# A two-layer decoder trunk: copying L's blocks out with ScalarE, moving bonus and gate into the units, and taking GpSimd's products to VectorE

## The chip, the cores and the metric

The kernel runs on one core of a Trainium2 chip as a single program. The metric is the device time of one execution in microseconds (us). A core has four engines that compute (TensorE for matrix products and transposes, VectorE, ScalarE and GpSimd for elementwise work), a fifth, SyncE, whose queue issues the transfers, and 16 DMA engines that carry them. Each engine works through its own list of instructions in order and waits for the others by semaphores.

## What is computed

The reference is a trunk of two layers over 256 tokens of width 2048, all in float32. The change touches only the mixer of the even layer. Its group A is an RWKV-7 recurrence with 16 heads of 64, its group B a sliding-window attention with 16 query heads on 2 key heads, and one output projection takes both.

```python
h = x @ e_w_in                        # r, k, v | decay, a, gate | q, k, v of attention
h = h + (token_shift(h) - h) * mu     # group A only
def wkv7_step(state, inp):            # one token: a_t = -kk, b_t = kk * a
    sa = einsum('bhij,bhj->bhi', state, a_t)
    state = state * w_t + sa[..., None] * b_t + v_t[..., None] * k_t
    return state, einsum('bhij,bhj->bhi', state, r_t)
y = scan(wkv7_step)
y = (y - mean(y)) * rsqrt(var(y) + WKV_GN_EPS) * gn_w + gn_b
bonus = sum(r * k * r_k, -1) * v      # per head
ya = (y + bonus) * g                  # the gate
yb = swa_sink_attention(q, k, v, sinks)
mix = concatenate([ya, yb]) @ e_w_out # then residual, LayerNorm, SwiGLU, LayerNorm, PLE
```

The odd layer (differential attention) and all that follows the even layer's output projection are the same before and after.

## The kernel before

Weights come from HBM in float32, two slabs of 128 rows by 512 columns at a time (a `raw` tile, 128x1024). `split_weights` makes two fp32r tiles of each: ScalarE casts `hi` (L109), VectorE subtracts `lo` (L110). The activations are split in the same way, and each product of the reference is three TensorE products here (`hi*xh`, `lo*xh`, `hi*xl`: L133 to L135 in `gemm`, L155 to L159 in `gemm_t`), called weight products below. So no weight product can run before ScalarE and then VectorE have done their part.

`wkv_operands` prepares the recurrence. Feature blocks f = 0 to 7 (two heads each) come in two halves, c = 0 and 1: per block the scaled operands `ar` and `bk` (L586 to L590), and after each second block the strictly lower 32x32 diagonal blocks of the matrix of `bk` times `ar`, written through the mask `m32` into the zeroed tile `blk` (L608: 16 masked copies of 32x128 per half, straight from PSUM). GpSimd makes three of the products of a block (L569, L589, L591). Then come the v projection (two gemms), the token shift of v by DMAs from `v` to `vs` (L627 to L629) with its two GpSimd operations and one VectorE operation per tile (L631 to L633), the mean removal (L638 to L640), and on GpSimd the bonus, the bias `gn_b`, the gate and the weight `gn_w` over whole tiles of 128x512 (L650 to L654). VectorE meanwhile transposes `blk` and inverts 128 triangular blocks of 32x32 by forward substitution (L665, L667: 60 operations), which gives `Tc` and `TTc`.

`wkv_chunks` is a generator of eight units: four groups of four heads, each with two chunks c of 128 tokens. A unit forms the masked matrices `lm4` (L706 on TensorE, L707 on VectorE, four of them), assembles the inverse `TT` from 32x32 blocks (GpSimd copies L711, TensorE L716 and L723, VectorE copies L719 and L726), and solves for `u` and `y` by a chain that passes between TensorE, ScalarE and VectorE (L729 to L781). L729 is its first product with `vs`; it and L741 need the v path and the inverse. A unit ends with the variance (L788 to L790), the scaling (L792), and two GpSimd operations that put in `gn_w` times gate and add to bonus (L793, L794).

`even_layer` writes four units, then the attention's projections (`swa_project`) and eight attentions (`swa_attend`), four of them between units. The order of the instructions on each engine is not the written one alone: a scheduler interleaves the lists, so weight products stand in the gaps of the units. Tiles come from pools, and a tile that takes over another's place waits for its last reader. In the end the eight heads' results are turned (`split_t`) and multiplied by `w_out` in two halves, first `ya`, whose sums wait in two tiles of 128x2048, then `yb`.

Of the kernel before, what the change touches and what calls it, by code (L numbers as in the profile page):

```python
# [9 lines left out]
F32 = mybir.dt.float32  # L10
# [8 lines left out]
P = 128  # L19
# [28 lines left out]
class Trunk:  # L48
# [24 lines left out]
    def more(self):  # L73

        pool = lambda n, b: self.ctx.enter_context(self.tc.tile_pool(name=n, bufs=b))
        self.rings.append(pool("wx", 3))
        self.rp = pool("rows", 2)
        self.ep = pool("emb", 1)
# [85 lines left out]
    def split_t(self, src, tag, pool):  # L164

        nc = self.nc
        ps = self.sm.tile([P, 2, SEQ], F32, name="s")
# [197 lines left out]
def even_layer(T, a, src):  # L365
# [4 lines left out]
    with ExitStack() as ctx:  # L370
        ev = ctx.enter_context(tc.tile_pool(name="ev", bufs=1))
        with tc.tile_pool(name="prep", bufs=1) as pr, T.psum(4, 4):
            ops, xT = wkv_operands(T, src, w_in, a, ev, pr)
            y = ops[-1]
        with tc.tile_pool(name="pairs", bufs=2) as pp, T.psum(2, 4, 2):
            units = wkv_chunks(T, ev, pp, *ops)
            for _ in range(4):
                next(units)
# [3 lines left out]
            yb = [None] * 4  # L382
            for u in range(4):
                next(units)
                swa_attend(T, pp, u, yb, *qkv)
            next(swa)
            for f in range(4, 8):
                swa_attend(T, pp, f, yb, *qkv)
            ya = [T.split_t([y[t][:, j * 256:(j + 1) * 256] for t in range(NT)], f"x{j}", T.xt) for j in range(4)]
            sums = [pp.tile([P, D], F32, name=f"lmat{t}", bufs=1) for t in range(NT)]  # L390
            for c in range(4):
                acc = T.gemm(ya, w_out, c * 512, rows=range(0, 8, 2))
                for t in range(NT):
                    nc.scalar.copy(out=sums[t][:, c * 512:(c + 1) * 512], in_=acc[t])
            x = T.load_x(src)
            for c in range(4):
                acc = T.gemm(yb, w_out, c * 512, rows=range(8, 16, 2), tail=2 if c == 3 else 0)
                for t in range(NT):
                    cs = slice(c * 512, (c + 1) * 512)
                    nc.vector.scalar_tensor_tensor(out=x[t][:, cs], in0=x[t][:, cs], scalar=ALPHA,  # L400
                                                   in1=sums[t][:, cs], op0=ALU.mult, op1=ALU.add)
# [4 lines left out]
def wkv_operands(T, src, w_in, a, ev, pr):  # L406
# [106 lines left out]
    late = tc.tile_pool(name="late", bufs=1)  # L513
# [12 lines left out]
    bview = blk.rearrange("p t (g c f r) -> p g r f c t", c=2, f=2, r=2)  # L526
    c2 = lambda u: u.rearrange("p (c t) -> p c t", t=P)
    ft = lambda n: lt.tile([P, SEQ], F32, name=n, bufs=4)
    bs = [pr.tile([P, AH], F32, name=f"bs{t}") for t in range(NT)]
    for c in range(2):  # L530
# [30 lines left out]
        for i in range(4):  # L561
# [7 lines left out]
            nc.gpsimd.tensor_tensor(out=bv, in0=kk[i], in1=av[i], op=ALU.mult)  # L569
# [19 lines left out]
            nc.gpsimd.tensor_tensor(out=bk[:, :, 0], in0=c2(bv), in1=en, op=ALU.mult)  # L589
            nc.vector.tensor_tensor(out=bk[:, :, 1], in0=c2(k[i]), in1=en, op=ALU.mult)  # L590
            nc.gpsimd.tensor_tensor(out=kk[i], in0=r, in1=k[i], op=ALU.mult)  # L591
# [472 lines left out]
```

## Time and profile before

| | before |
|---|---|
| median of 3 runs | 2655.54 us (2654.8 to 2657.75) |
| the profiled execution | 2654.55 us |
| its span, first to last instruction | 2652.9 us |
| TensorE busy | 2585.4 us, 97% of the span |
| VectorE, ScalarE, GpSimd busy | 1492.6, 1138.9, 121.9 us |
| granted TensorE clock, mean | 0.983 |

All durations below are from the profiled execution; what lies outside its span is 1.65 us. The granted clock is given as a share of 2.4 GHz; at 1.2 GHz, the lower of the two levels, it is 0.5, and a stretch with 0.71 has been partly at one and partly at the other. A weight product's busy time overlaps that of the next one, so counts of products are multiplied with the distance between two starts. The part that the change touches ends at about 563 us of the span.

### The profile page before, as it was taken

What the parts mean: (1) busy time and instruction counts of PE and PEld (TensorE: products, weight loads), DVE (VectorE), ACT (ScalarE), POOL (GpSimd) and SP (SyncE); (2) the same over time, 40 slices, a digit from 0 to 9 for tenths busy, and PEclk for the clock granted to TensorE, in tenths of its full rate; (3) what the DMA queues carried; (4) which work ended last, traced back from release to release, by engine and by line L of the source; (5) the groups of instructions that cost most, each with busy time, mean ns of one, the idle gap of its engine ahead of it and who ended that gap; (6) DMA issues with size and microseconds to landing.
All of it is one profiled execution on the core that took longest, in us unless ns stands there. A gap on an engine that the chain in (4) does not pass through costs nothing.

```text
span 2652.9 us, 32574 instructions
## 1 busy us (share of the span) xinstructions
PE 2585.4 (97%) x12509; PEld 2097.4 (79%) x12509; DVE 1492.6 (56%) x2072; ACT 1138.9 (43%) x1493; POOL 121.9 (5%) x190
## 2 busy tenths in 40 slices
PE   8998799999999999999999999999999999999999
PEld 6877576678888888888888777777888888888877
DVE  4779535675445444445666565567545444545574
ACT  5443224544444344443445454444444433444343
POOL 0113421000000000000000000000000000000000
PEclk9998879999999999999999999999999999999999
DMA  6335312566666666666565555556666666666654
GB/s 192 108 113 151 96 33 76 161 194 210 190 190 186 195 195 191 190 190 190 179 224 183 159 159 167 169 173 209 189 190 190 191 191 195 187 190 190 192 174 166
DMA packets 240282, 458.56 MB, mean 173 GB/s; under 512 B 15280, under 2 KB 20066, under 8 KB 240126
## 3 DMA queue, kind: packets, MB, share of 16 engines
q1 hardware_dynamic: 240126, 456.48, 56.7%
q8 instruction: 98, 1.61, 0.3%
q14 instruction: 58, 0.48, 0.1%
HBM read 453.28 MB, written 2.10 MB: 172 GB/s over the span
## 4 chain that ended last, share of the span: by engine, by line
PE 88%; DVE 6%; POOL 2%; DMA 2%; ACT 1%; issue 1%; SPq 0%; ACTq 0%; POOLq 0%; DVEq 0%
PE acc L133 26%; PE acc L134 26%; PE acc L135 26%; DVE lo L110 2%; PE acc L155 1%; PE acc L159 1%; PE acc L157 1%; PE s L170 1%; PE sx L860 1%; ACT hi L109 1%; DVE blk L608 0%; PE s L729 0%; DVE lmat L707 0%; DMA lnb<-in_ln_b_dram 0%; PE s L934 0%
## 5 line engine op out<-in xcount | busy, mean ns | idle before, releaser
L110 DVE TENSOR_TENSOR lo<-raw,hi 128x1024 fp32r<-128x1024 f32 (+2 forms) x840 | 1022.7, 1219 | 961.8 <-ACT hi L109 960.0
L109 ACT CAST hi<-raw 128x1024 fp32r<-128x1024 f32 (+2 forms) x840 | 877.1, 1045 | 1200.9 <-PE acc L135 1088.6
L133 PE MATMUL acc<-hi,x0h 128*128 128x512 f32 (+1 forms) x292 | 120.6, 413 | 0.7 <-ACT x0h L176 0.7
L134 PE MATMUL acc<-lo,x3h 128*128 128x512 f32 (+1 forms) x292 | 115.4, 395 | 4.5 <-DVE lo L110 4.5
L134 PE MATMUL acc<-lo,x4h 128*128 128x512 f32 (+1 forms) x292 | 115.9, 397 | 3.1 <-DVE lo L110 3.1
L135 PE MATMUL acc<-hi,x0l 128*128 128x512 f32 (+1 forms) x292 | 118.5, 406 | 0.0
L134 PE MATMUL acc<-lo,x2h 128*128 128x512 f32 (+1 forms) x292 | 114.8, 393 | 2.5 <-DVE lo L110 2.5
L134 PE MATMUL acc<-lo,x0h 128*128 128x512 f32 (+1 forms) x292 | 117.0, 401 | 0.1
L133 PE MATMUL acc<-hi,x4h 128*128 128x512 f32 (+1 forms) x292 | 115.5, 397 | 1.6 <-DVE x L242 1.6
L133 PE MATMUL acc<-hi,x1h 128*128 128x512 f32 (+1 forms) x292 | 116.2, 398 | 0.0
L133 PE MATMUL acc<-hi,x3h 128*128 128x512 f32 (+1 forms) x292 | 115.6, 396 | 0.0
L135 PE MATMUL acc<-hi,x3l 128*128 128x512 f32 (+1 forms) x292 | 115.4, 395 | 0.0
L134 PE MATMUL acc<-lo,x5h 128*128 128x512 f32 (+1 forms) x292 | 114.5, 392 | 0.8 <-DVE lo L110 0.8
L135 PE MATMUL acc<-hi,x4l 128*128 128x512 f32 (+1 forms) x292 | 115.1, 394 | 0.0
L133 PE MATMUL acc<-hi,x2h 128*128 128x512 f32 (+1 forms) x292 | 114.7, 393 | 0.0
L135 PE MATMUL acc<-hi,x2l 128*128 128x512 f32 (+1 forms) x292 | 114.7, 393 | 0.0
L135 PE MATMUL acc<-hi,x1l 128*128 128x512 f32 (+1 forms) x292 | 114.4, 392 | 0.0
L134 PE MATMUL acc<-lo,x1h 128*128 128x512 f32 (+1 forms) x292 | 114.4, 392 | 0.0
L134 PE MATMUL acc<-lo,x6h 128*128 128x512 f32 (+1 forms) x292 | 114.1, 391 | 0.2 <-DVE lo L110 0.2
L134 PE MATMUL acc<-lo,x7h 128*128 128x512 f32 (+1 forms) x292 | 114.1, 391 | 0.0
L133 PE MATMUL acc<-hi,x5h 128*128 128x512 f32 (+1 forms) x292 | 114.1, 391 | 0.0
L133 PE MATMUL acc<-hi,x6h 128*128 128x512 f32 (+1 forms) x292 | 114.0, 390 | 0.0
(561 smaller groups left out, 5184.8 us busy)
## 6 DMA issues: line engine op xcount, KB each, us to landing
raw<-in_ffn_w_dram SPq DMA_DIRECT2D x528, 512.0 KB, 3.6
raw<-in_o_w_in_dram SPq DMA_DIRECT2D x96, 512.0 KB, 3.9
raw<-in_e_w_in_dram SPq DMA_DIRECT2D x64, 512.0 KB, 3.6
raw<-in_ple_w_gate_dram SPq DMA_DIRECT2D x64, 512.0 KB, 4.4
raw<-in_e_w_out_dram SPq DMA_DIRECT2D x32, 512.0 KB, 3.6
raw<-in_o_w_out_dram SPq DMA_DIRECT2D x32, 512.0 KB, 4.0
x<-in_x_dram SPq DMA_DIRECT2D x16, 256.0 KB, 5.6
lng<-in_ln_g_dram SPq DMA_DIRECT2D x16, 256.0 KB, 3.0
```

Source lines behind the costliest of these rows:

```text
L109: nc.scalar.copy(out=hi, in_=raw)
L110: nc.vector.tensor_tensor(out=lo, in0=raw, in1=hi.bitcast(F32), op=ALU.subtract)
L133: nc.tensor.matmul(o, xh[:, kk, s], hi[:, kk], start=k == 0, stop=False)
L134: nc.tensor.matmul(o, xh[:, kk, s], lo[:, kk], start=False, stop=False)
L135: nc.tensor.matmul(o, xl[:, kk, s], hi[:, kk], start=False, stop=k == 2 * n - 1)
L155: nc.tensor.matmul(o, hi[:, kk, fs], xh[:, kk], start=k == 0 and i % 2 == 0, stop=False, skip_group_check=True)
L157: nc.tensor.matmul(o, lo[:, kk, fs], xh[:, kk], start=False, stop=False, skip_group_check=True)
L159: nc.tensor.matmul(o, hi[:, kk, fs], xl[:, kk], start=False, stop=k == nk - 1, skip_group_check=True)
L170: nc.tensor.transpose(ps[:, kk, t * P:(t + 1) * P], src[t][:, kk * P:(kk + 1) * P], self.ident)
L860: nc.tensor.matmul(ps, qT[s, c, f % 4, t * P:(t + 1) * P], kT[c][s, 0:nk * P], start=True, stop=True)
```

## The change

- **Blocks of L.** `L608` becomes `nc.scalar.copy` without a mask into a second tile `L` (after, L627). One masked copy over the whole 128x1024 tile (after, L662) then moves the wanted parts into the zeroed `blk`.
- **GpSimd's products.** L569, L589 and L591 and both shift operations L631 and L633 are VectorE's (after, L588, L608, L610, L649, L651).
- **Bonus and gate.** L650 to L654 are gone. Each unit does them for its own four heads and chunk, all on VectorE: bonus, bias, weight, sum and gate (after, L806 to L811), in place of L793 and L794. The two vectors come by four DMAs at the head of each second group into a tile that takes over `blk0`'s place.
- **Order.** Two units are written ahead of the attention's projections where it was four, and attentions are spread between the units.
- **Output product.** The halves are `ya0, ya1, yb0, yb1` and then `ya2, ya3, yb2, yb3`, with two transposes (`turn`) ahead of each, in buffers of the weight products' pool; the sums of the first half lie in tiles of the places of `ar0` to `ar3` and `bk0` to `bk3`.
- **Pools.** Four pools get `reuse_waits="tile"`.

```diff
+    L = ev.tile([P, 32, 32], F32, name="blk1")
+    bview = L.rearrange("p t (g c f r) -> p g r f c t", c=2, f=2, r=2)
...
-            nc.gpsimd.tensor_tensor(out=bv, in0=kk[i], in1=av[i], op=ALU.mult)
+            nc.vector.tensor_tensor(out=bv, in0=kk[i], in1=av[i], op=ALU.mult)
...
-                    nc.vector.copy_predicated(bview[q, g, par], m32[q, None, None, :].to_broadcast([32, 2, NT, 32]),
-                                              pl[q, :, :, q])
+                    nc.scalar.copy(out=bview[q, g, par], in_=pl[q, :, :, q])
...
-            nc.gpsimd.tensor_tensor(out=vs[t][:, cs], in0=vs[t][:, cs], in1=v[t][:, cs], op=ALU.subtract)
+            nc.vector.tensor_tensor(out=vs[t][:, cs], in0=vs[t][:, cs], in1=v[t][:, cs], op=ALU.subtract)
...
-    for c in range(2):
...
-            nc.gpsimd.tensor_tensor(out=v3[t][:, h], in0=v3[t][:, h],
-                                    in1=bs[t][:, h, None].to_broadcast([P, 8, HD]), op=ALU.mult)
-            nc.gpsimd.tensor_tensor(out=v[t][:, cs], in0=v[t][:, cs], in1=gnb, op=ALU.add)
-            nc.gpsimd.tensor_tensor(out=v[t][:, cs], in0=v[t][:, cs], in1=gate[t][:, cs], op=ALU.mult)
-            nc.gpsimd.tensor_tensor(out=gate[t][:, cs], in0=gate[t][:, cs], in1=gnw, op=ALU.mult)
...
+    nc.vector.copy_predicated(blk, m32[:, :, None].to_broadcast([P, 32, 32]), L)
...
+        if g % 2 == 0:
+            gn = ev.tile([P, 2, 2, G * HD], F32, name="blk0")
+            for j, vec in enumerate((a["e_gn_w"][0], a["e_gn_b"][0])):
+                for e in range(2):
+                    o = (g + e) * G * HD
+                    nc.sync.dma_start(out=gn[:, e, j], in_=vec[o:o + G * HD].partition_broadcast(P))
...
-            nc.gpsimd.tensor_tensor(out=yf, in0=yf, in1=q1[c][:, gs], op=ALU.mult)
-            nc.gpsimd.tensor_tensor(out=q2[c][:, gs], in0=q2[c][:, gs], in1=yf, op=ALU.add)
+            bonus = ysq.rearrange("p g d -> p (g d)")
+            nc.vector.tensor_tensor(out=ysq, in0=v[c][:, gs].rearrange("p (g d) -> p g d", d=HD),
+                                    in1=bs[c][:, G * g:G * g + G, None].to_broadcast([P, G, HD]), op=ALU.mult)
+            nc.vector.tensor_tensor(out=bonus, in0=bonus, in1=gn[:, g % 2, 1], op=ALU.add)
+            nc.vector.tensor_tensor(out=yf, in0=yf, in1=gn[:, g % 2, 0], op=ALU.mult)
+            nc.vector.tensor_tensor(out=yf, in0=yf, in1=bonus, op=ALU.add)
+            nc.vector.tensor_tensor(out=v[c][:, gs], in0=yf, in1=gate[c][:, gs], op=ALU.mult)
...
+                acc = T.gemm([ya[0], ya[1], yb[0], yb[1]], w_out, c * 512, rows=(0, 2, 8, 10))
...
+                acc = T.gemm([ya[2], ya[3], yb[2], yb[3]], w_out, c * 512, rows=(4, 6, 12, 14), tail=2 if c == 3 else 0)
```

The order of the instructions shows the change in three places. A row is a line of the program, an operation, what it writes and reads, and the size; xN stands for N of them in a row.

On VectorE at the end of the second half of `wkv_operands` this stood before; the eight L608 there are the last of the half's sixteen, `bk` holds the last block's product, and L658 is the transpose ahead of the forward substitution:

```order
L572 TENSOR_TENSOR k<-k,a 128x256
L583 TENSOR_TENSOR ew_1896<-ew_1896,ee 128x1
L608 COPY_PREDICATED blk_536<-m_531,s 32x2x2x32
L590 TENSOR_TENSOR bk_1902<-k,en 128x2x128
L608 COPY_PREDICATED blk_536<-m_531,s 32x2x2x32 x7
L614 COPY bs_538<-s 128x8
L614 COPY bs_539<-s 128x8
L110 TENSOR_TENSOR lo<-raw,hi 128x1024 x2
L658 STREAM_TRANSPOSE blk_2297<-blk_536 128x1024
L110 TENSOR_TENSOR lo<-raw,hi 128x1024
```

and this stands there now (bk, k, kk: the last block's products, L662: the masked copy, L664: the transpose):

```order
L608 TENSOR_TENSOR bk_1903<-b,en 128x2x128
L609 TENSOR_TENSOR bk_1903<-k,en 128x2x128
L610 TENSOR_TENSOR kk<-r,k 128x256
L110 TENSOR_TENSOR lo<-raw,hi 128x1024
L632 COPY bs_539<-s 128x8
L632 COPY bs_540<-s 128x8
L110 TENSOR_TENSOR lo<-raw,hi 128x1024
L662 COPY_PREDICATED blk_536<-m_531,blk_538 128x1024
L664 STREAM_TRANSPOSE blk_538<-blk_536 128x1024
L110 TENSOR_TENSOR lo<-raw,hi 128x1024
```

The masked copies that stood between the last block's products and the transpose are gone; one copy of 128x1024 and two products of 128x256 have come in.

GpSimd's list was this before, from the shift of v's second half of columns in the second token tile on (`brow` holds `gn_b` or `gn_w`):

```order
L631 TENSOR_TENSOR vs_1941<-vs_1941,v_1939 128x512
L633 TENSOR_TENSOR v_1939<-vs_1941,v_1939 128x512
L650 TENSOR_TENSOR v_1938<-v_1938,bs_538 128x512 x2
L652 TENSOR_TENSOR v_1938<-v_1938,brow 128x512
L653 TENSOR_TENSOR v_1938<-v_1938,gate_440 128x512
L654 TENSOR_TENSOR gate_440<-gate_440,brow 128x512
L650 TENSOR_TENSOR v_1939<-v_1939,bs_539 128x512 x2
L652 TENSOR_TENSOR v_1939<-v_1939,brow 128x512
L653 TENSOR_TENSOR v_1939<-v_1939,gate_441 128x512
L654 TENSOR_TENSOR gate_441<-gate_441,brow 128x512
L652 TENSOR_TENSOR v_1938<-v_1938,brow 128x512
```

and now, from the setting up of the units' masks on (`x_2627` is the attention's, `mf` and `lmat` are the units'):

```order
L82 AFFINE_SELECT x_2627<-x_2627 128x128 x2
L689 MEMSET mf 128x512
L699 MEMSET TT_2395 128x512
L82 AFFINE_SELECT mf<-mf 128x2x128 x2
L698 MEMSET lmat_2394 128x2048
L699 MEMSET TT_2396 128x512
L723 COPY TT_2395<-blk_2275 32x4x32 x4
L779 MEMSET S_2496 128x256
L723 COPY TT_2396<-blk_2275 32x4x32 x4
```

The whole v path has left GpSimd, and its setting up of the units' tiles stands at the front.

On VectorE, where the first unit ends (L788 to L792 before) and the next unit's masked matrices begin (L707 before), the order was:

```order
L788 TENSOR_REDUCE var<-ysq 128x4
L707 COPY_PREDICATED lmat_2417<-mask,s 128x512
L789 TENSOR_SCALAR var<-var 128x4
L707 COPY_PREDICATED lmat_2417<-mask,s 128x512
L792 TENSOR_TENSOR y<-y,var 128x256
L707 COPY_PREDICATED lmat_2417<-mask,s 128x512 x2
L719 COPY pm<-s 32x128 x2
L726 COPY TT_2419<-s 32x4x32 x2
```

and is now, with L719 for the masked matrices and L806 to L811 for bonus and gate:

```order
L800 TENSOR_REDUCE var<-ysq 128x4
L719 COPY_PREDICATED lmat_2394<-mask,s 128x512
L801 TENSOR_SCALAR var<-var 128x4
L806 TENSOR_TENSOR ysq<-v_1939,bs_539 128x256
L804 TENSOR_TENSOR y<-y,var 128x256
L808 TENSOR_TENSOR ysq<-ysq,blk_2401 128x256
L809 TENSOR_TENSOR y<-y,blk_2401 128x256
L719 COPY_PREDICATED lmat_2394<-mask,s 128x512
L810 TENSOR_TENSOR y<-y,ysq 128x256
L719 COPY_PREDICATED lmat_2394<-mask,s 128x512
L811 TENSOR_TENSOR v_1939<-y,gate_440 128x256
L719 COPY_PREDICATED lmat_2394<-mask,s 128x512
```

Between the first and the last of the next unit's four masked matrices stand seven operations of the ending unit, where it was two.

## Rows read from the trace of the kernel before

**Rows 1.** Windows by stage: stretch, length; busy TensorE, weight loads, VectorE, ScalarE, GpSimd; clock.

```profile
97.90:124.00 26.10, 21.23 (x120) 16.52 (x119) 23.19 (x42) 10.85 (x23) 11.31 (x12) 0.80 0.20 54
124.00:169.80 45.80, 45.80 (x356) 42.49 (x356) 28.83 (x36) 22.51 (x29) 0.00 (x0) 1.00 0.52 154
169.80:238.90 69.10, 60.82 (x270) 46.14 (x269) 64.64 (x114) 27.43 (x41) 17.98 (x16) 0.93 0.39 112
238.90:298.00 59.10, 42.74 (x211) 33.82 (x209) 45.34 (x62) 12.72 (x19) 38.65 (x35) 0.71 0.44 130
298.00:430.50 132.50, 124.61 (x994) 91.44 (x993) 57.53 (x154) 39.41 (x97) 30.05 (x48) 0.88 0.14 40
430.50:563.30 132.80, 130.58 (x662) 95.99 (x660) 86.27 (x207) 66.97 (x140) 2.48 (x3) 1.00 0.51 160
```

**Rows 2.** GpSimd by lines, 244 to 300 us: busy, mean ns, idle before.

```profile
L653 POOL TENSOR_TENSOR v<-v,gate 128x512 f32<-128x512 f32 x4 | 6.9, 1749 | 0.2
L650 POOL TENSOR_TENSOR v<-v,bs 128x512 f32<-128x512 f32 x4 | 6.0, 1525 | 1.2 <-DVE vs L640 1.2
L652 POOL TENSOR_TENSOR v<-v,brow 128x512 f32<-128x512 f32 x4 | 5.6, 1412 | 4.7 <-DMA brow<-in_e_gn_b_dram 4.7
L654 POOL TENSOR_TENSOR gate<-gate,brow 128x512 f32<-128x512 f32 x4 | 5.4, 1362 | 0.2
```

**Rows 3.** Timeline of GpSimd: the first operation after the v products.

```profile
244.98 1.26 POOL L631 TENSOR_TENSOR vs<-vs,v 128x512 f32<-128x512 f32 x1 [16.84 <-ACT hi L109]
```

**Rows 4.** VectorE by lines, 238 to 300 us.

```profile
L692 DVE MEMSET lmat<- 128x2048 f32 x1 | 1.8, 1765 | 4.1 <-POOL gate L654 4.1
```

**Rows 5.** Timeline of TensorE shortly before the first unit's chain.

```profile
288.80 0.32 PE L716 MATMUL s<-blk,lmat 32*32 32x32 f32 x4 [7.02 <-POOL TT L711]
```

**Rows 6.** VectorE by lines, end of the first half, 97.9 to 127 us.

```profile
L608 DVE COPY_PREDICATED blk<-m,s 32x128 f32<-32x128 uint8 x15 | 11.0, 731 | 0.2
...
L590 DVE TENSOR_TENSOR bk<-k,en 128x256 f32<-128x256 f32 x4 | 3.4, 846 | 0.0
```

**Rows 7.** VectorE by lines and shapes, 300 to 560 us.

```profile
L110 DVE TENSOR_TENSOR lo<-raw,hi 128x1024 fp32r<-128x1024 f32 x42 | 51.2, 1222 | 32.5 <-ACT hi L109 32.1
L707 DVE COPY_PREDICATED lmat<-mask,s 128x512 f32<-128x512 uint8 x28 | 19.5, 724 | 8.5 <-PE s L706 8.3
...
L242 DVE TENSOR_TENSOR x<-x,acc 128x512 f32<-128x512 f32 x6 | 3.8, 680 | 0.0
L792 DVE TENSOR_TENSOR y<-y,var 128x256 f32<-128x256 f32 x8 | 3.4, 425 | 3.8 <-POOL var L790 3.7
```

**Rows 8.** ScalarE by lines and shapes, 300 to 560 us.

```profile
L890 ACT CAST x4h<-sx 128x128 fp32r<-128x128 f32 x4 | 1.0, 269 | 5.6 <-PE acc L134 4.5 <-PE sx L886 1.1
```

**Rows 9.** Timeline of VectorE in the forward substitution, where GpSimd starts beside it.

```profile
216.85 0.40 DVE L667 TENSOR_TENSOR blk<-blk,tmp 128x234 f32<-128x234 f32 x1
...
218.75 1.50 DVE L667 TENSOR_TENSOR blk<-blk,tmp 128x238 f32<-128x238 f32 x1
```

**Rows 10.** Windows of the weight products of line L134 alone, one of three.

```profile
263.80:297.96 34.16, 10.40 (x21) 5.05 (x20) 0.71 0.41 125
...
331.63:356.74 25.11, 2.76 (x5) 1.38 (x5) 0.58 0.08 22
373.95:391.81 17.86, 3.18 (x7) 1.32 (x7) 0.96 0.10 31
391.81:411.41 19.60, 2.71 (x6) 1.34 (x6) 0.86 0.19 56
```

**Rows 11.** Timeline of TensorE in the output product: start, duration.

```profile
562.21 0.39 PE L135 MATMUL acc<-hi,x7l 128*128 128x512 f32 x1
562.44 0.39 PE L133 MATMUL acc<-hi,x7h 128*128 128x512 f32 x1
```

**Rows 12.** Timeline of TensorE between the second and third unit.

```profile
326.88 0.28 PE L716 MATMUL s<-blk,lmat 32*32 32x32 f32 x4 [0.39 <-DVE lmat L707]
...
328.47 0.28 PE L716 MATMUL s<-blk,lmat 32*32 32x32 f32 x4 [0.87 <-DVE lmat L707]
```

More of the change, by code (lines that the diff above doesn't have):

```diff
@@ L370, in even_layer, with unit, turn @@
     with ExitStack() as ctx:
-        ev = ctx.enter_context(tc.tile_pool(name="ev", bufs=1))
+        ev = ctx.enter_context(tc.tile_pool(name="ev", bufs=1, reuse_waits="tile"))
         with tc.tile_pool(name="prep", bufs=1) as pr, T.psum(4, 4):
             ops, xT = wkv_operands(T, src, w_in, a, ev, pr)
[L374 to L378, printed above, removed]
+            y = ops[-2]
+        with tc.tile_pool(name="pairs", bufs=2, reuse_waits="tile") as pp, T.psum(2, 4, 2):
+            units = wkv_chunks(T, a, ev, pp, *ops)
+            ya, yb = [None] * 4, [None] * 4
+            def unit(n):
+                for _ in range(n):
+                    next(units)
+            def turn(j):
+                ya[j] = T.split_t([y[t][:, j * 256:(j + 1) * 256] for t in range(NT)], f"x{j}", T.xt,
+                                  T.mm.tile([P, 2, SEQ], F32, name="acc"))
+            unit(2)
             swa = swa_project(T, pp, xT, w_in, a)
@@ L381, in even_layer @@
             next(swa)
[L382 to L385, printed above, removed]
+            swa_attend(T, pp, 0, yb, *qkv)
+            unit(1)
+            swa_attend(T, pp, 1, yb, *qkv)
+            unit(1)
+            swa_attend(T, pp, 2, yb, *qkv)
             next(swa)
-            for f in range(4, 8):
+            unit(1)
+            swa_attend(T, pp, 3, yb, *qkv)
+            for f in range(4, 7):
+                unit(1)
                 swa_attend(T, pp, f, yb, *qkv)
-            ya = [T.split_t([y[t][:, j * 256:(j + 1) * 256] for t in range(NT)], f"x{j}", T.xt) for j in range(4)]
-            sums = [pp.tile([P, D], F32, name=f"lmat{t}", bufs=1) for t in range(NT)]
+            swa_attend(T, pp, 7, yb, *qkv)
+            turn(0)
+            turn(1)
+            sums = [[ev.tile([P, 512], F32, name=("ar", "bk")[t] + str(c)) for c in range(4)] for t in range(NT)]
             for c in range(4):
-                acc = T.gemm(ya, w_out, c * 512, rows=range(0, 8, 2))
+                acc = T.gemm([ya[0], ya[1], yb[0], yb[1]], w_out, c * 512, rows=(0, 2, 8, 10))
                 for t in range(NT):
-                    nc.scalar.copy(out=sums[t][:, c * 512:(c + 1) * 512], in_=acc[t])
+                    nc.scalar.copy(out=sums[t][c], in_=acc[t])
+            turn(2)
+            turn(3)
             x = T.load_x(src)
             for c in range(4):
-                acc = T.gemm(yb, w_out, c * 512, rows=range(8, 16, 2), tail=2 if c == 3 else 0)
+                acc = T.gemm([ya[2], ya[3], yb[2], yb[3]], w_out, c * 512, rows=(4, 6, 12, 14), tail=2 if c == 3 else 0)
                 for t in range(NT):
@@ L510, in wkv_operands @@
     T.rotary_tables(a["positions"][0])
-    late = tc.tile_pool(name="late", bufs=1)
+    late = tc.tile_pool(name="late", bufs=1, reuse_waits="tile")
     lt = late.__enter__()
```

27 lines of the change are left out of this document (10 added, 17 removed).

## The prediction

> **What bounds the kernel now.** I read the page's table of slices first, for where TensorE is not full, then cut that stretch into stages by the windows, and in each stage looked for what TensorE waits for. Past 563 us nothing is changed. The clock and TensorE's busy time divide the rest [rows 1]. From 97.9 to 124 us VectorE is busy for 23.19 of 26.10 us: it bounds the end of the first half of `wkv_operands`. From 124 to 169.8 TensorE has no gap and its full clock; what VectorE saves there is worth nothing. From 169.8 to 238.9 us VectorE is busy for 64.64 of 69.10, so it bounds the second half, forward substitution included. The v products end at 238.9; only at 298.0 does the first unit's chain start (L729), a stage of 59.1 us in which GpSimd is busy for 38.65. Here the v path ends last: GpSimd's four lines of bonus and gate take 6.9 + 6.0 + 5.6 + 5.4 = 23.9 us and 4.7 us of waiting for `gn_b` [rows 2]; its first operation behind the shift's DMAs starts at 244.98, 6.1 us after the last v product [rows 3]. VectorE stands behind it: the zeroing of `lmat` waits 4.1 us for L654 [rows 4], and TensorE waits 7.02 us for the copies of `TT`, which GpSimd can make only then [rows 5]. The granted clock is 0.71. From 298 to 430.5 seven units follow, TensorE busy for 124.61 of 132.5 at a clock of 0.88, then the last unit, attention and the output product at the full clock.
>
> So three stages bear on this change: two that VectorE bounds and one that GpSimd bounds. VectorE loses work in the first two, and takes GpSimd's in all.
>
> **A, end of the first half: -4 us (0 to -6).** A masked copy costs 0.731 us, the four L590, which run beside GpSimd, 0.846 each [rows 6]; an operation of that shape costs 0.425 where GpSimd is idle [rows 7]. Eight of the sixteen copies stand ahead of the half's last block in VectorE's order; they go: -8 x 0.731 = -5.85. The other eight end what the next stage needs less. GpSimd's contention goes from L590: -4 x 0.42 = -1.7. One `lo` (1.222) moves behind: -1.2. Twelve products come in: 12 x 0.425 = +5.1. Sum -3.7, taken as -4. ScalarE's price for a copy of 32x128 from PSUM is not in the trace; the nearest is its cast of 128x128, 0.269 [rows 8], and I take 0.27 for it, since the elements per partition are the same. It has 10.85 busy us of 26.1 here, so eight copies (2.2) find room. The upper bound is that they cost what VectorE's do, 0.73, and stand in the chain: then 0. The lower one is -6, if half the products fall into VectorE's gaps.
>
> **B, second half to the last v product: -7.5 us (-3 to -11).** Gone are 16 x 0.731 = 11.7, contention at L590, 1.7, and that of the forward substitution: beside GpSimd a 0.40 us operation took 1.50 [rows 9], and four such cost 4 x 1.10 = 4.4 us more. New are the twelve products, 5.1; one masked copy of 128x1024, no row, estimated at twice the 0.724 of 128x512, 1.45; and four shift operations of the first half of v, 4 x 0.68 = 2.7 [rows 7]. Sum: -17.8 + 9.3 = -8.5. The masked copy stands at the head of the forward substitution and now waits for ScalarE's last eight copies, behind which the transpose and all sixty operations are queued: +1. That gives -7.5. Bounds: -11 if the masked copy runs no longer than a plain operation of its size (1.222), waits for nothing, and gaps of VectorE hide the four shift operations, -3 if the sixteen copies stay on the path at 0.27 each (4.3).
>
> **C, last v product to the first unit's second step: -31 us (-23 to -36).** GpSimd's 23.9 us, and the 4.7 for `gn_b`, leave the path. What ends last now is VectorE's list behind the shift's DMAs: 6.1 us until they land, as before [rows 3]; then six shift operations and five `lo` of half width, 11 x 0.68 = 7.5; two transposes, two reductions and two subtractions of 128x1024, 6 x 1.22 = 7.3; the zeroing, 1.77 [rows 4]; mask cast and the two small scalings, estimated at 0.7 each pair, 1.4; four masked matrices, 4 x 0.724 = 2.9 [rows 7]. Together 27.0 us, and 1 for the small products up to L741: 28 instead of 59.1, so -31. The copies of `TT`, which cost 7.02 [rows 5], now find GpSimd free. What would be late next is this list itself. -23 if GpSimd's setting up of the units' tiles slows seven of these operations as it did in the forward substitution, 7 x 1.10 = 7.7 [rows 9]; -36 if four `lo` or shift operations and a transpose fit into the 6.1 us of landing.
>
> **D, what the wait had covered: +14.6 us.** In 263.8 to 298 the scheduler had put attention's q products: 20 of L134, and of its two sister lines as many [rows 10], 60 together. They start 0.23 us apart at the full clock (562.21 to 562.44) [rows 11]: 13.8 us, plus half that distance for seven products of half width, 0.8. That work doesn't vanish with the stall. The shorter stall still leaves some at its head, so this is a full price; C minus D is what the stage is worth.
>
> **E, the clock: -2 us (-9 to +10).** After the stall the clock was low in two units [rows 10]: the one from 331.63 took 25.11 us at 0.58, one from 373.95 with two more of L134, six products, 17.86 at 0.96. The difference is 7.25, with the six products 8.6; I take 8, for the former holds a part of an attention. The unit at 0.86 lost 19.60 - 17.86 = 1.7. So 9.7 us are to be had, and -9 is that. As a hole ahead of the units stays, and their gaps too, I expect one unit at the low level again: 8 of the 9.7 stay, -2. The other bound, +10, is 9.7 once more.
>
> The Trainium skill weighs this otherwise: its page "TensorE: Matmul & The Clock Gate", section "HAM oscillation — how this bites in real kernels", has the penalty as half of the throttled time. The unit at 0.58 was at the low level for 84% of its 25.11 us, 21 us, so by the page it lost 10.5, not 8; E's bounds would be some 2.5 wider and the sum the same. The row decides, as part of the unit waits for other engines, whose speed the clock leaves alone.
>
> **F, VectorE between the units: +4 us (0 to +12).** Six operations of 128x256 end a unit on VectorE where it was one, and five of them stand between the next unit's masked matrices, 5 x 0.425 = 2.1 us: its last masked matrix comes that much later. TensorE waited 0.39 and 0.87 us for masked matrices before [rows 12]; three weight products put between cover 0.7. 1.4 more in five transitions, 7.0, less the 1.3 waited before in two, 2.6: +4. Zero if weight products cover all; 2.1 x 6 = 12 or more if none. GpSimd's two operations per unit were off the path and save nothing.
>
> **G, turns in the weight products' buffers: +1.4 (0 to +4).** Each of the four turns holds one of two accumulators, for which the next product must wait until a copy and a subtraction of 128x512 have read it, 2 x 0.68 [rows 7]; that is exposed once.
>
> At nothing: the four `gn` loads wait on SyncE's queue for the second of the last two transposes, and the weights behind them wait too, but the four `raw` tiles already loaded hold 12 products each, 4 x 12 x 0.23 = 11 us, and the shift's DMAs landed within 6.1 [rows 3]; without that cover the whole wait, up to 6 us, would show. The output product keeps its number of products and sums, and the pool settings remove waits only.
>
> **Sum.** -4 - 7.5 - 31 + 14.6 - 2 + 4 + 1.4 = -24.5. Against the profiled execution, 2654.55, that is 2630; the median shown stands 1.0 above it, so 2631. All best ends give -47.4, all worst ends +14.6.
>
> **Rivals.** *More gain, about -40: 2615.* VectorE's new operations all fall into gaps (F and G 0), A and B reach -6 and -9, the clock is full in the units (E -9): -6 - 9 - 31 + 14.6 - 9 = -40.4. For it: in the units VectorE is busy for only 57.53 of 132.5 us [rows 1]. Against: it is the order, not the load, that makes TensorE wait there [rows 12].
> *The copies only change engine, -13: 2642.* ScalarE's copies cost as VectorE's did and the masked copy waits for them, so A and B vanish, and the change doesn't do what it says: -24.5 + 11.5 = -13. For it: sixteen small pieces per half. Against: the cast at 0.269 [rows 8].
> *Slower: the low clock stays through the units, 2687.* A unit at the low level costs 8 us more; seven more units than the forecast's one, 7 x 8 = 56, turn -24.5 into +31.5. It decides from the fourth further unit on (24.5 / 8 = 3.1). For it: TensorE's gaps between the units grow by F. Against: before, behind a stage at 0.71, the seven units came to 0.88 together [rows 1].
>
> **How the numbers follow.** The forecast's case (-18 to -33) has 0.50, more gain 0.22, the copies that only change engine 0.18, a time within 0.2% (5.3 us, about what a measurement of this kernel can tell from no change) 0.04, the slower one 0.06. Faster: 0.50 + 0.22 + 0.18 = 0.90. The range reaches down to 2609, nearly all best ends, since one reason, an idle VectorE, could bring several of them; 2646 (-9.5) takes in most of the third case and leaves out the last two and what of the third is above.
>
> **What would show it.** L729 of the first unit (now L741) some 28 us behind the last v product; GpSimd nearly idle there; the stage up to the v products 61 to 62 us; no 1.50 us operations in the forward substitution; the twelve products at 0.42; TensorE's waits for the masked matrices (L719) up by 1 to 1.5 us in five transitions; one unit at a clock near 0.6. Wrong would make it: ScalarE's copies at 0.7, the clock at its low level over several units, or `gn` loads that hold up weights.

## The result and the profile after

The changed kernel takes 2626.53 us (median of 6 runs, 2620.67 to 2641.72) against 2655.17 for the kernel before (median of 6, 2651.03 to 2658.80). The ratio is 0.9896, its 95% interval 0.9868 to 0.9925. The forecast was 2631. A second set of 6 runs, taken later beside others, gave 2630.59 (2623.76 to 2639.85), a ratio of 0.991 (0.9891 to 0.9929). Over all 12 runs the median is 2628.7.

The profiled execution took 2621.11 us with a span of 2619.4, so it lies at the low end of the six: 33.4 us under the profiled execution of before, where the medians differ by 28.6. The same stages as in [rows 1], cut at the same events (columns as there):

```profile
98.10:119.30 21.20, 19.40 (x125) 15.77 (x124) 15.65 (x44) 13.97 (x33) 0.00 (x0) 0.92 0.25 69
119.30:164.60 45.30, 45.30 (x352) 41.99 (x352) 24.75 (x30) 25.16 (x37) 0.00 (x0) 1.00 0.54 155
164.60:222.50 57.90, 56.22 (x272) 44.12 (x270) 50.94 (x111) 33.06 (x57) 0.53 (x1) 1.00 0.47 133
222.50:249.00 26.50, 16.72 (x124) 15.28 (x123) 25.02 (x46) 6.30 (x9) 10.13 (x14) 0.81 0.47 133
249.00:437.80 188.80, 176.26 (x1288) 127.06 (x1286) 107.71 (x313) 70.51 (x171) 20.55 (x34) 0.96 0.26 76
437.80:529.80 92.00, 88.09 (x452) 67.37 (x451) 58.66 (x112) 42.57 (x75) 1.05 (x1) 1.00 0.57 177
```

The lengths go from 26.1 to 21.2 (end of the first half, -4.9), 45.8 to 45.3, 69.1 to 57.9 (second half, -11.2), 59.1 to 26.5 (last v product to the first unit, -32.6), and 265.3 to 280.8 for all that follows up to 530 (+15.5). Behind it both kernels take 2089.6 us. The differences add up to -33.7, so nothing outside these stages moved. In the first and the third of these rows TensorE is now idle for only 1.8 and 1.7 us (4.9 and 8.3 before), so it sets their length, and no longer VectorE; its own busy time there fell by 1.8 and 4.6 us, at a clock of 0.92 for 0.80 and of 1.00 for 0.93. GpSimd, busy 38.65 us in the fourth stage before, has 10.13 left there; TensorE, which was at 0.71 of its clock in it, is at 0.81 for a stage less than half as long.

The copies and the products beside GpSimd at the end of the first half before, in the window of [rows 1]:

```profile
L608 DVE COPY_PREDICATED blk<-m,s 32x128 f32<-32x128 uint8 x11 | 8.0, 725 | 0.1
...
L590 DVE TENSOR_TENSOR bk<-k,en 128x256 f32<-128x256 f32 x4 | 3.4, 846 | 0.0
L588 DVE TENSOR_TENSOR ar<-r,ee 128x256 f32<-128x256 f32 x4 | 2.8, 691 | 0.0
L572 DVE TENSOR_TENSOR k<-k,a 128x256 f32<-128x256 f32 x4 | 2.3, 566 | 1.2 <-ACT a L570 1.2
L586 DVE SCALAR_TENSOR_TENSOR ar<-kk,ee 128x256 f32<-128x256 f32 x4 | 2.2, 552 | 0.8 <-ACT ee L579 0.8
```

What VectorE and ScalarE pay there now, and for the masked copy in the second half (groups by line; answers to [rows 6] and [rows 8]; ScalarE's line has the copies of both halves):

```profile
L588 DVE TENSOR_TENSOR b<-kk,a 128x256 f32<-128x256 f32 x4 | 1.7, 420 | 0.0
...
L605 DVE SCALAR_TENSOR_TENSOR ar<-kk,ee 128x256 f32<-128x256 f32 x4 | 1.7, 419 | 0.0
...
L610 DVE TENSOR_TENSOR kk<-r,k 128x256 f32<-128x256 f32 x4 | 1.7, 415 | 0.0
```

```profile
L662 DVE COPY_PREDICATED blk<-m,blk 128x1024 f32<-128x1024 uint8 x1 | 1.4, 1354 | 1.4 <-ACT blk L627 1.4
```

```profile
L627 ACT COPY blk<-s 32x128 f32<-32x128 f32 x32 | 12.1, 379 | 5.0 <-PE s L623 4.6
```

The same products in the second half before, beside GpSimd:

```profile
L590 DVE TENSOR_TENSOR bk<-k,en 128x256 f32<-128x256 f32 x4 | 3.5, 864 | 0.0
...
L588 DVE TENSOR_TENSOR ar<-r,ee 128x256 f32<-128x256 f32 x4 | 2.8, 688 | 0.0
L586 DVE SCALAR_TENSOR_TENSOR ar<-kk,ee 128x256 f32<-128x256 f32 x4 | 2.7, 684 | 0.8 <-ACT ee L579 0.8
L572 DVE TENSOR_TENSOR k<-k,a 128x256 f32<-128x256 f32 x4 | 2.2, 548 | 1.3 <-ACT a L570 1.3
```

The new products cost 0.42 us each, as estimated, and L605, the old L586 (0.684 there), costs the same. ScalarE's copy of a block takes 0.379 us where 0.27 was assumed. The masked copy took 1.354 us and waited 1.4 for ScalarE.

TensorE's waits from the first unit to the end of the output product, before and after (waiting line, what it waited for, us in all, times, longest):

```profile
PE s L716 <- DVE lmat L707: 6.3, 11, 1.0
PE acc L133 <- DVE x L242: 1.6, 3, 0.9
```

```profile
PE s L728 <- DVE lmat L719: 11.0, 6, 2.5
PE acc L133 <- DVE x2l L177: 1.6, 1, 1.6
PE acc L133 <- DVE x L242: 1.1, 3, 0.4
```

One of these waits, first on VectorE, then on TensorE (timelines):

```profile
316.66 0.73 DVE L719 COPY_PREDICATED lmat<-mask,s 128x512 f32<-128x512 uint8 x1
317.28 0.15 DVE L801 TENSOR_SCALAR var<-var 128x4 f32<-128x4 f32 x1
317.34 0.42 DVE L806 TENSOR_TENSOR ysq<-v,bs 128x256 f32<-128x256 f32 x1
318.66 0.43 DVE L804 TENSOR_TENSOR y<-y,var 128x256 f32<-128x256 f32 x1 [0.90 <-POOL var L802]
319.00 0.42 DVE L808 TENSOR_TENSOR ysq<-ysq,blk 128x256 f32<-128x256 f32 x1
319.34 0.42 DVE L809 TENSOR_TENSOR y<-y,blk 128x256 f32<-128x256 f32 x1
319.67 0.72 DVE L719 COPY_PREDICATED lmat<-mask,s 128x512 f32<-128x512 uint8 x1
320.28 0.42 DVE L810 TENSOR_TENSOR y<-y,ysq 128x256 f32<-128x256 f32 x1
320.61 0.73 DVE L719 COPY_PREDICATED lmat<-mask,s 128x512 f32<-128x512 uint8 x1
```

```profile
320.44 0.28 PE L728 MATMUL s<-blk,lmat 32*32 32x32 f32 x4 [2.06 <-DVE lmat L719]
```

The first masked matrix of the next unit comes at 316.66, the second only at 319.67. Between them stand five operations of the ending unit, and VectorE itself waits 0.90 us for L802, GpSimd's power of -1/2 for the variance, with the masked matrices queued behind. TensorE waits 2.06 us for it.

### The profile page after: what moved, and what is told of

It reads as the page before. It is cut to its first block, busy times and chain, and to the rows that moved or that the text cites. A ratio compares the mean times of both kernels' runs of the same rounds, so it can differ in the third digit from the quotient of the medians.

```text
span 2619.4 us, 32555 instructions
## 1 busy us (share of the span) xinstructions
PE 2562.2 (98%) x12509; PEld 2082.6 (80%) x12509; DVE 1470.6 (56%) x2113; ACT 1151.0 (44%) x1525; POOL 53.6 (2%) x126
## 4 chain that ended last, share of the span: by engine, by line
PE 90%; DVE 5%; DMA 2%; ACT 2%; issue 1%; POOL 1%; SPq 0%; ACTq 0%; POOLq 0%; DVEq 0%
PE acc L135 26%; PE acc L134 26%; PE acc L133 26%; DVE lo L110 1%; PE acc L155 1%; PE acc L159 1%; PE acc L157 1%; PE s L170 1%; ACT hi L109 1%; PE sx L877 1%; DMA raw<-in_e_w_in_dram 0%; PE s L951 0%; PE s L741 0%; DMA lnb<-in_ln_b_dram 0%; DVE x L223 0%
## 5 line engine op out<-in xcount | busy, mean ns | idle before, releaser
L134 PE MATMUL acc<-lo,x3h 128*128 128x512 f32 (+1 forms) x292 | 114.7, 393 | 11.0 <-DVE lo L110 11.0
L134 PE MATMUL acc<-lo,x4h 128*128 128x512 f32 (+1 forms) x292 | 115.3, 395 | 0.6 <-DVE lo L110 0.6
L134 PE MATMUL acc<-lo,x0h 128*128 128x512 f32 (+1 forms) x292 | 115.4, 395 | 0.0
L134 PE MATMUL acc<-lo,x1h 128*128 128x512 f32 (+1 forms) x292 | 115.1, 394 | 0.0
L134 PE MATMUL acc<-lo,x2h 128*128 128x512 f32 (+1 forms) x292 | 114.7, 393 | 0.0
L134 PE MATMUL acc<-lo,x6h 128*128 128x512 f32 (+1 forms) x292 | 114.0, 390 | 0.0
L134 PE MATMUL acc<-lo,x5h 128*128 128x512 f32 (+1 forms) x292 | 113.7, 389 | 0.0
L134 PE MATMUL acc<-lo,x7h 128*128 128x512 f32 (+1 forms) x292 | 113.6, 389 | 0.0
L135 PE MATMUL acc<-hi,x5l 128*128 128x512 f32 (+1 forms) x292 | 113.4, 388 | 0.0
## 6 DMA issues: line engine op xcount, KB each, us to landing
x<-in_x_dram SPq DMA_DIRECT2D x16, 256.0 KB, 4.7
lng<-in_ln_g_dram SPq DMA_DIRECT2D x16, 256.0 KB, 3.2
```

The source lines that it names most:

```text
L134: nc.tensor.matmul(o, xh[:, kk, s], lo[:, kk], start=False, stop=False)
L135: nc.tensor.matmul(o, xl[:, kk, s], hi[:, kk], start=False, stop=k == 2 * n - 1)
```

## The experiments

Every kernel was timed in five rounds beside the kernel before. Names with `a_` are the changed kernel with one thing undone or added, names with `b_` the kernel before with one part of the change. "Clock" is the mean over a kernel's runs of the granted clock of the whole execution. Where stages are compared, the times come from one profiled execution each; the medians of two variants can be told apart only where they differ by more than the changed kernel's two sets of runs do (2626.53 and 2630.59) and their ranges hardly overlap.

| kernel | median us (range) | ratio to before (95%) | clock |
|---|---|---|---|
| changed kernel | 2626.53 (2620.67 to 2641.72) | 0.9896 (0.9868 to 0.9925) | 0.991 |
| a_again | 2630.59 (2623.76 to 2639.85) | 0.991 (0.9891 to 0.9929) | 0.990 |
| a_blocks_on_vector | 2642.74 (2641.75 to 2644.67) | 0.9957 (0.9945 to 0.9969) | 0.988 |
| b_blocks_on_scalar | 2646.55 (2641.91 to 2651.65) | 0.9964 (0.9953 to 0.9975) | 0.987 |
| b_bonus_in_units | 2650.01 (2646.18 to 2658.65) | 0.9988 (0.9977 to 0.9998) | 0.984 |
| a_products_on_gpsimd | 2633.32 (2627.81 to 2637.90) | 0.992 (0.9907 to 0.9934) | 0.991 |
| a_order_of_before | 2624.16 (2621.71 to 2640.85) | 0.9898 (0.9877 to 0.9919) | 0.991 |
| a_pools_of_before | 2630.05 (2622.66 to 2635.75) | 0.9907 (0.9892 to 0.9922) | 0.990 |
| a_tail_deferred | 2636.94 (2625.55 to 2645.09) | 0.9931 (0.991 to 0.9952) | 0.984 |
| a_bonus_on_gpsimd | 2642.67 (2637.38 to 2644.47) | 0.995 (0.9938 to 0.9962) | 0.985 |
| a_filled | 2651.18 (2646.38 to 2656.16) | 0.9981 (0.9968 to 0.9993) | 0.984 |
| a_deferred_filled | 2635.54 (2632.59 to 2648.89) | 0.9934 (0.9914 to 0.9953) | 0.985 |
| a_deferred_order_of_before | 2619.89 (2616.02 to 2634.78) | 0.9875 (0.9848 to 0.9902) | 0.991 |

**The blocks, undone and alone.** Undone in the changed kernel:

```diff
-                    nc.scalar.copy(out=bview[q, g, par], in_=pl[q, :, :, q])
+                    nc.vector.copy_predicated(bview[q, g, par], m32[q, None, None, :].to_broadcast([32, 2, NT, 32]), pl[q, :, :, q])
...
-    nc.vector.copy_predicated(blk, m32[:, :, None].to_broadcast([P, 32, 32]), L)
```

> The changed kernel, but L's blocks are again copied by VectorE through the mask, 32 masked copies of 32x128, and the copy of 128x1024 is gone. Theory (VectorE's list sets the end of both halves): eight copies of 0.73 us return in the first half, sixteen in the second, 17.5 us; the masked copy of 1.35 and its wait for ScalarE of 1.4 go, so the two stages grow by 14 to 15 us and the kernel stands at 2640 us instead of 2626. Rival (the copies were in gaps, the gain of these stages came from GpSimd's silence alone): 2627, within 3.

The two halves end at 234.4 us instead of 222.1 (here and below the start of the last v product), 12.3 later, and the median is 16 higher than the first set's, 12 higher than the second's; none of its five runs is as quick as the slowest of the 12: the copies were on the path. The same edit alone in the kernel before:

> The kernel before with one part alone: L's blocks copied by ScalarE and masked once. Theory (VectorE sets the end of both halves, and what follows moves along): the first half ends 6 us sooner, the last v product 14 to 16 sooner, and the wait behind it stays at 59 us: 2639. Rival (GpSimd, unchanged here, holds its part: its three products per block become what the halves wait for): less than half of that, 2648 or more.

The last v product comes at 233.1, 5.7 us sooner, not 14 to 16; the median is 9 lower. That is nearer to the rival: with GpSimd's products still in place the move is worth 9 us, as the last step of the full change 12 to 16.

**Bonus and gate alone** in the kernel before (L650 to L654 out, L806 to L811 and the `gn` loads in):

> The kernel before with one part alone: bonus, bias and gate inside the units on VectorE, all other products on GpSimd as before, blocks, order and output product as before. Theory (the v path set the start of the units): the first unit's L729 comes some 24 us sooner than at 298; of it 11 us go to q products that must be done later and 4 to 5 to VectorE's work between the units, the clock gives some 3 back: 2643 us. Rival 1 (this part is the whole gain): 2628. Rival 2 (the wait only moves to the token shift on GpSimd): 2652.

Here the forecast of 2643 fell; rival 2 is the nearest in time but not in its place. Stages behind the last v product:

```profile
239.00:266.60 27.60, 18.08 (x134) 15.57 (x133) 25.40 (x42) 7.78 (x12) 13.52 (x19) 0.90 0.51 153
266.60:557.80 291.20, 273.46 (x1730) 198.79 (x1729) 166.50 (x422) 111.60 (x243) 21.24 (x35) 0.93 0.34 104
```

The wait shrinks to 27.6 us, as much as in the full change. But the stretch up to the end of the output product grows from 264.9 to 291.2. 59 products (156 before the first unit in the old kernel, 97 here) come later, 59 x 0.23 = 13.6 us, the waits for masked matrices rise from 6.3 to 9.8 and TensorE's other waits by some 4, and the clock of the stretch is 0.93 for 0.94. The products and the waits make up some 21 of the 26.3 us; how much of the rest is the clock's is not known. A wait that other work fills is worth little when it goes.

**GpSimd's products back**, in the changed kernel (five `nc.vector` to `nc.gpsimd`: L588, L608, L610, L649, L651):

> The changed kernel with the three products of each block and the two shift operations on GpSimd again. Theory (an operation of VectorE beside GpSimd is slower): VectorE is spared 5.1 us in each half, but pays 4.4 in each for its other products and about 4 in the forward substitution, and the v path ends 3 us later: 2630 us, the first half's end within 1 us of the changed kernel's, the second half's 3 us later. Rival (VectorE's load alone counts): the halves end 10 us sooner in all, 2617.

The halves end at 167.4 and 232.4 instead of 165.0 and 222.1, so VectorE, with 5 us less to do in each, is later, and by more than the theory had (2.4 and 10.3 us, for 1 and 3). Its lines in the second half:

```profile
L609 DVE TENSOR_TENSOR bk<-k,en 128x256 f32<-128x256 f32 x4 | 3.8, 948 | 0.0
L607 DVE TENSOR_TENSOR ar<-r,ee 128x256 f32<-128x256 f32 x4 | 2.8, 689 | 0.0
L591 DVE TENSOR_TENSOR k<-k,a 128x256 f32<-128x256 f32 x4 | 2.7, 666 | 1.7 <-ACT a L589 1.7
```

They cost 0.41 to 0.42 us in the changed kernel. The slowing is not the only way in which GpSimd's products cost time: they are also waited for. TensorE's waits for them in the second half, first in this kernel, then in the kernel before; in the changed kernel, where VectorE makes them, it waits 0.4 us:

```profile
PE s L623 <- POOL bk L608: 2.4, 2, 1.2
```

```profile
PE s L604 <- POOL bk L589: 2.1, 3, 1.2
```

Which of the two is worth more was not separated. The stage behind is 3.3 us shorter (23.6), against what was expected, so the first unit starts at 256.0 us, 7 later than in the changed kernel (249.0). The median, 2633.32, is 7 above the changed kernel's first set and 3 above the second, which by itself is hardly clear of the spread.

**Order and pools of before**, each alone undone in the changed kernel:

> The changed kernel with the order of before in the even layer: four units, projections, four units with four attentions, four attentions, the four turns in the small buffers, the output product by ya and yb. Theory (order and halves are worth little): 2626 within 4, the waits for masked matrices still near 11 us. Rival (spreading the attentions fills the gaps between the units and holds the clock): 2634 or more, with a lower clock in the units.

> The changed kernel without the setting of the four pools that is new. Theory (no buffer is waited for on the path): 2626, within 3, and the first unit starts where it does now, at 249 us. Rival (tiles that take over the places of earlier ones hold the units' start): the first unit starts 4 us later or more, as the zeroing of lmat did before, 2632.

2624 and 2630: neither can be told from the changed kernel. (The second edit took the setting from the pools of TensorE's results too, which had it before the change.) The waits for masked matrices are 10.6 us in the former, and the first unit starts at 249.5 and 251.6.

**The tail of a unit.** To shorten the waits at L728, the operations L804 to L811 of a unit are written behind the next unit's `TT` copies:

```diff
+            if todo:
+                finish(*todo)            # L804 to L811 of the unit before
             pz = T.sm.tile([P, G, HD], F32, name="s")
...
+            todo = (g, c, gs, gn, y, ysq, var)
```

> The changed kernel, but a unit's scaling, bonus, weight and gate are written behind the next unit's TT copies, so that fewer of them stand between its masked matrices (three or four instead of seven). Theory (these operations hold TensorE between the units): TensorE's waits for masked matrices fall from 11.0 us to 6 to 8, the clock in the units is no lower, and the kernel takes 2622 us instead of 2626. Rival (the wait moves to the operations behind, or the clock decides): waits for other results grow by as much, 2626 or more.

```profile
PE s L741 <- DVE lmat L732: 3.6, 6, 1.1
PE s L741 <- DVE sum L900: 2.8, 2, 1.4
PE sx L907 <- DVE prob L902: 2.2, 3, 1.3
```

The waits for masked matrices fell from 11.0 to 3.6 us, more than expected; others came up (2.8 us for the sums of an attention, L900), so that TensorE's waits fell from 16.2 to 12.0 in all. Yet the median is 10 above the changed kernel's first set and 6 above the second; the times overlap. What is clear of the spread is the clock: 0.984 (0.981 to 0.989) for 0.990 over the 12 runs. At the price of the clock found below, 2.2 us for 0.001, these six thousandths are some 13 us; by this estimate the kernel would be 3 to 7 us quicker than the changed one at one clock, where its waits are 4.2 us shorter. Why the clock is lower here stays open: the stretches at the low level have weight products (L134 alone, one of three lines):

```profile
360.00:370.00 10.00, 1.88 (x3) 1.00 (x3) 0.50 0.01 2
430.00:440.00 10.00, 1.20 (x3) 0.69 (x3) 0.53 0.01 2
```

Putting two of the tail's operations on GpSimd instead (L806, L808) did not help either:

> The changed kernel with the unit's two operations for the bonus and the bias (L806 and L808) on GpSimd. Theory (order on VectorE between the units decides): two operations of 0.43 us fewer between the masked matrices, 0.85 us in five transitions, 4 us, of which slower operations beside GpSimd take half back: 2624. Rival (GpSimd's price for VectorE's operations is the larger): the masked matrices take 1 us or more each beside it, 2632.

2642.67, with a clock of 0.985 and 11.3 us of waits, slower than the rival, but not by the rival's price. The masked matrices cost 0.721 us as before. Five to six thousandths of clock, some 11 to 13 us, are most of the 12 to 16 us by which it is slower than the changed kernel; the scaling suffers too, as does its wait for L802, which now stands behind the bonus in GpSimd's list (VectorE by lines; in the changed kernel L804 took 3.4 us and waited 7.2):

```profile
L719 DVE COPY_PREDICATED lmat<-mask,s 128x512 f32<-128x512 uint8 x28 | 20.1, 721 | 0.5 <-PE s L718 0.4
...
L804 DVE TENSOR_TENSOR y<-y,var 128x256 f32<-128x256 f32 x8 | 6.0, 752 | 10.1 <-POOL var L802 10.1
```

**The clock.** If the clock falls behind TensorE's waits, work put into them should hold it:

```diff
+            full = T.sm.tile([P, 4 * P], F32, name="s")
+            for _ in range(8):
+                nc.tensor.matmul(full, xT[0][0][:, 0, 0:P], xT[0][0].rearrange("p k t -> p (k t)"), start=True, stop=True)
+            pq = full[:, 0:G * 32].rearrange("p (g c) -> p g c", c=32)
```

> The changed kernel with eight products of 128x512 per unit whose result nobody reads, written into the buffer of L728's result just ahead of it, where TensorE waits for the masked matrices (11.0 us in all). Theory (the granted clock falls behind these waits, and about 1.8 us of time hang on 0.001 of its mean): the fillers take 8 x 0.23 = 1.8 us of a wait of 1.8 to 2.5 and cost next to nothing, the clock is 0.994 or more in every run, and the kernel takes 2618 to 2622 us. Rival (the low clock has another cause): the clock stays at 0.985 to 0.994 as in the changed kernel's six runs, and the fillers cost up to 8 us: 2627 to 2635.

> The kernel with the deferred tail (waits for masked matrices 3.6 us in its profile, clock 0.981 to 0.989 over its runs) with four such fillers per unit. Theory (as for eight fillers): the clock rises to 0.992 or more, and since the waits were shorter the kernel takes 2615 to 2622. Rival (the low clock in it does not come from waits for masked matrices): the clock stays under 0.989, 2630 or more.

> The changed kernel again, for the spread of its clock beside the two others on the same chip. If its runs differ by chance, the mean clock is again 0.990 to 0.992 and the median 2624 to 2631; if the deferred tail's low clock was a matter of the chip and the hour, it is 0.987 or less here, 2633 or more.

The theory fell. The fillers cut the waits to 4.9 us and the kernel takes 2651, longer than the rival had too, with a clock of 0.984 in the mean of its runs. In a_deferred_filled the waits are 2.2 us, the clock is 0.985 and the median 2635.54, as its rival had it. a_filled's last two units show how. All engines first, then L134 alone (one of the three lines of weight products), in the same two stretches; after the second fence, L134 from there to the end of the output product:

```profile
390.00:416.00 26.00, 24.27 (x135) 18.68 (x136) 9.33 (x37) 5.45 (x19) 2.98 (x6) 0.54 0.00 1
420.00:442.00 22.00, 21.02 (x134) 16.75 (x135) 7.20 (x29) 6.89 (x23) 1.11 (x1) 0.53 0.00 1
```

```profile
390.00:416.00 26.00, 0.00 (x0) 0.00 (x0) 0.54 0.00 1
420.00:442.00 22.00, 0.00 (x0) 0.00 (x0) 0.53 0.00 1
```

```profile
442.00:552.00 110.00, 46.69 (x119) 22.38 (x119) 1.00 0.51 161
```

The clock is at its low level nearly throughout, TensorE is busy for 24.27 of 26 us and 21.02 of 22, and not one weight product is among this work. They have moved: L134 has not one product from 360 to 442 us, and 119 behind that. In a_deferred_filled it has none from 360 to 430. That the scheduler counted the fillers and gave TensorE's free places otherwise is the likely reason; no run shows it. In the changed kernel the units have them:

```profile
389.33:412.48 23.15, 4.04 (x9) 1.69 (x9) 1.00 0.15 45
412.48:437.82 25.34, 4.46 (x8) 1.89 (x8) 0.87 0.15 45
```

a_again, run on the same chip beside the two filled kernels, has a clock of 0.990, so the hour or the chip did not make their difference. Its profile shows something else, too: the same program, with the same 11.0 us of waits, had its units at 0.90 where the first profile had 0.96. Weight products within the units don't by themselves hold the clock. The last run puts the deferred tail into before's order, in which the q products follow four units and so each unit has some beside it:

> The kernel with before's order of units and of the output product (2624 us, clock 0.985 to 0.994) with the deferred tail added. Theory (shorter waits gain some 4 us at one clock, and the clock falls longer where the units have few weight products beside them; this order keeps weight products for every unit): waits for masked matrices from 10.6 to about 4 us, mean clock 0.990 to 0.992, 2619 to 2625. Rival (the deferred tail itself lowers the clock, wherever the weight products stand): mean clock under 0.987, 2632 or more.

Its waits are 5.6 us instead of 10.6, its clock 0.991, and its median 2619.89 the lowest of all, 4.3 below the same order without the deferral. The ranges overlap; with the clocks alike, some 4 to 5 us agrees with what the deferral is worth at one clock in the other order. The rival, that the deferral itself lowers the clock wherever it stands, is out. Why the clock is lower with it in the changed kernel's order is not shown.

## Why the prediction was right, point by point

The sum of -24.5 became -28.6 by the medians of the first set, -24.4 by those of the second, and -33.4 by the profiled executions, on which the terms stand.

- **A, -4 (0 to -6):** -4.9. The size was right, its working in part by luck. VectorE's busy time fell by 7.5 us (23.19 to 15.65), twice the 3.7 of the sum: 8.0 us of copies left the stretch and not 5.85, and GpSimd's contention was on four lines and not on L590 alone, 4 x 0.98 = 3.9 for 1.7; the `lo` that was to move behind stayed, three in either window. Not all of it came through, as TensorE, busy for 19.40 of 21.20 us, now sets the length. ScalarE's price (0.379 for 0.27) changed nothing in the sum, which had no term for it.
- **B, -7.5 (-3 to -11):** -11.2, just outside. The term that was mis-sized is the contention: only L590 was counted. L586 (0.684), L588 (0.688) and L572 (0.548) ran beside GpSimd too, and all cost 0.42 after: with L590 (0.864) 4 x 1.1 = 4.4 us and not 1.7. The 4.4 for the forward substitution (60 operations took 24.1 us before, 19.8 after), the 11.7 for the copies, the masked copy (1.354 for 1.45) and its wait (1.4 for 1) came as written. That makes -10.2. The rest may be the waits of TensorE for GpSimd's products (2.1 us at L604), which the sum did not have.
- **C, -31 (-23 to -36):** -32.6. The list behind the v products took 26.5 us for 28. The shift's first operation on VectorE starts 5.4 us behind the last v product (227.94), the zeroing took 1.77, the transposes, reductions and subtractions 1.2 each but one of 1.9; the mask cast and the small scalings, for which there was no row, took 0.7 and not 1.4. GpSimd was not nearly idle, as the signs had it, but busy for 10.13 us with the units' tiles and the copies of `TT`. The hole that stays is TensorE's 9.78 us ahead of 239.07 us.
- **D, +14.6:** +14.6. 89 weight products before the first unit for 156: 60 of 512 columns, 60 x 0.23, and seven of 256 at half that, as in the forecast. b_bonus_in_units shows the term alone.
- **F, +4 (0 to +12):** waits for masked matrices from 6.3 to 11.0, +4.7. The size is right, one cause was missed: VectorE's own wait for L802, 7.2 us over the eight units (3.7 for L790 before).
- **G, +1.4:** the product behind a turn waited 1.6 us for L177.
- **E, -2 (-9 to +10):** the term that was least known, and it is the reason for the difference between profile and median. The units were at the low level for 31.8 us before (132.5 us at 0.88: 132.5 x 0.12 x 2), for 15 after (188.8 at 0.96). At 0.42 us for each in the changed kernel and 0.28 to 0.42 in the one before (both estimates, below) that is -3 to -7 in the first profiled execution. In a_again's, the same program, the units were at the low level for 40 us (200.0 at 0.90): +3 to +8. So -2 lies between what two executions of one kernel gave, and that it fits the median is luck; its argument looked at gaps alone, and a_filled and a_again show that gaps alone don't decide.

The terms so measured, with the 0.5 us of the second stage, add up to -31 to -35, the stages to -33.7.

Of the rivals, "the copies only change engine" is refuted by a_blocks_on_vector. "More gain" was near in the quickest runs (2621), by B and E, not by F falling away. The low clock through the units did not come here, but for two stretches of 26 and 22 us it came in a_filled, so its chance was not idle.

The change doesn't have one main cause. Undoing the blocks costs 12 to 16 us, undoing the products' move puts the first unit 7 us later (3 to 7 by the medians), and the bonus in the units, whose stage moved most (-31.5), is worth some 4 alone (by its interval 0.5 to 6). What it is worth in the changed kernel was not run.

## What to carry to other kernels

When a wait goes, ask first what filled it: here 67 products that were done in it moved behind it, and 14.6 of its 32.6 us came back as their price. When work is moved between two engines that slow each other, count every operation that runs beside, not the dearest alone. And in a stage in which TensorE's small products alternate with large ones, compare kernels over several runs with their clocks beside them: an order with shorter waits (11.0 to 3.6 us for the masked matrices) came out 6 to 10 us slower at a clock of 0.984, and in another order of the units, at 0.991, some 4 us quicker.

## What the runs showed of the hardware

VectorE's operations of 128x256 took 0.41 to 0.42 us alone and up to 0.95 (L609) in the stretches in which GpSimd worked beside them: four lines in the kernel before (0.55 to 0.86 in each half), three of them in the second half of a_products_on_gpsimd (0.67 to 0.95), and not one alone.

The granted clock differs between runs of one kernel (the changed one: 0.985 to 0.994), and the time with it. Take each run's time and clock against its kernel's mean: over all 149 runs (those of the table and of the kernel before) a straight line gives 1.84 us for 0.001 of clock, but that mixes two prices. The 68 runs of the changed kernel and its variants give 2.2, the 81 of the kernel before and its two variants 1.5, each within 0.2. 0.001 of some 2640 us is 5.3 us at the low level, so 1 us there costs 0.42 us in the former and 0.28 in the latter. The two profiles of the changed kernel agree: at the same waits the part from the first unit to the end of the output product took 281.0 us at 0.98 and 294.0 at 0.92. Added up over stretches of 1 us, it was at the low level for 13.7 and 44.4 us: 13.0 us of time for 30.7, again 0.42. The Trainium skill's page "TensorE: Matmul & The Clock Gate" (section "HAM oscillation — how this bites in real kernels") puts the penalty at half of the throttled time; the runs give less. That in part of these stretches TensorE waits for other engines is a likely reason, which no run separates.

The clock fell behind a wait of TensorE in the changed kernel's units (2.06 us ahead of 320.44, then 0.57 from 322 to 326). How long it stayed low was another matter: in a_filled it stayed for most of 26 and 22 us in which TensorE was busy with the units' small products alone, and was at 1.00 from 442 us on, where the weight products were. In a_tail_deferred it was at the low level for 10 us with weight products among the work, too (0.50 from 360 to 370). Why two runs of one kernel differ was not settled.
